# Hybrid decoder step in two-part float32: which engine makes the weights' low parts and the sums of squares

## The chip, the cores and the metric

One core of one Trainium2 chip runs the whole program. The metric is the device time of one execution in microseconds (us); the median of three runs is given. Engines are named as the profile names them: PE (TensorE), DVE (VectorE), ACT (ScalarE), POOL (GpSimd) and SP (the queue from which most transfers start).

## The reference

One inference step of a decoder of two layers, for a prompt of 1024 tokens and 8 sample tokens together (1032 columns), 1024 features, everything in float32. Each layer has two sublayers:

```python
h = modulate(rmsnorm(x, g_mix), sh1, sc1)
p = h @ w_in                      # 1024 -> 3072: q, k, v, g of 4 retention heads; u, vv of 4 gMLP groups
...                               # retention with rotary q/k and group norm; chunked spatial gating
x = x + gt1[:, None, :] * (concatenate([o_ret, o_gm], -1) @ w_out)
h2 = modulate(rmsnorm(x, g_ffn), sh2, sc2)
a, buf_new = causal_dwconv(h2 @ w_up, conv_buf, conv_w, conv_b)   # 1024 -> 4096, width 3
f = jax.nn.silu(a[..., :D_FF]) * a[..., D_FF:]
x = x + gt2[:, None, :] * (f @ w_down)                            # 2048 -> 1024
```

The shifts, scales and gates come from a small product `silu(c) @ w_ada` per layer. After the second layer a last rmsnorm gives the output; the retention states, the convolution states and some rows of the gMLP are outputs too.

## The kernel before

Features lie on the 128 partitions and tokens along the free axis, so X is 8 tiles of 128 x 1032. A product in float32 is made of three products in float32r: each operand is split into a high part (a copy rounded to float32r, made on ScalarE) and a low part (the operand less the high part), and high x high, high x low and low x high are added up in PSUM. `block` does that for one 128x128 weight tile over three token chunks of 344 columns: nine matmuls.

Weights arrive as 160 pieces of eight 128x128 tiles (128 x 1024 columns, 512 KB). The class `Weights` sends for them (`issue`, two pieces ahead, on SP's queue), splits them (`prepare`: the high part on ScalarE at L188, the low part on GpSimd at L189) and hands them out by units (`get`). `ahead` prepares one more piece of the unit that comes next, if it lacks one. It is called in `unit` after k-tiles 2, 4 and 6 of eight, in `partial` at the outputs from the fourth on, in `joint` once, and in `final_partial` after each group of outputs of the second and third chunk. Most units are one piece.

The order of all work is written out by hand, and every engine runs its instructions in that order. A main stream of matrix products runs through the layer; side work (rotary embedding, retention, gating, the convolution's taps) is cut into steps, and `side.tick` puts some between the products. A step says how long, in us of the main stream, the next is to be left alone.

- `unit`: one piece, eight k-tiles, 72 matmuls into one of two PSUM buffers of three banks. Its evacuation starts with a small copy on ScalarE (L596) and a product with the rows' scale on VectorE (L597). In the feed-forward part two ScalarE passes follow, then the taps L887 and the eight sample columns L891 on VectorE, Silu (L901) on ScalarE, the gate L911, and the split into `ahi` (L913) and `alo` (L915).
- `partial`: some k-tiles of a product back to the residual, for all eight outputs; VectorE adds each into X (L299, L305).
- `final_partial`: the last k-tiles of a sublayer, one token chunk after the other (order 2, 0, 1), outputs in groups of three, three and two. VectorE adds them into X (L508). `scaled` makes the next operand: Hh on ScalarE (L411), Hl on VectorE (L412); for output tile 0 ScalarE makes a copy first and GpSimd the low part (L409). `squares` squares each group on ScalarE (L334), and GpSimd adds the first two groups (L338). Then `norm` follows as a side task: `add_squares` adds what is left to one row per partition on VectorE (L345, L353, L357), `inv_rms` sums the row over partitions with four small matmuls (L365) and takes the inverse root on VectorE, and the result goes over DRAM to all partitions as R.
- `joint`: the first two units of the next sublayer, chunk by chunk, so that they can begin before the last chunk is normed; both are evacuated at its end. There are four joints, one per sublayer.
- At the start the same steps are done for X as loaded: `scaled` (no tile on GpSimd there), `squares` (first two chunks on GpSimd, L332, the third on ScalarE), `add_squares`, and between the chunks of the first joint (`start`) the norms and the first part of the conditioning.

Of the kernel before, what the change touches and what calls it, by code (L numbers as in the profile page):

```python
# [7 lines left out]
F32 = mybir.dt.float32  # L8
F32R = mybir.dt.float32r
# [8 lines left out]
NB = 8  # L18
# [13 lines left out]
# columns of the packed per-layer parameters  # L32
# [3 lines left out]
# The k-tiles of the two projections back to the residual, in groups that go into PSUM together.  # L36
# Mixing: 0-3 retention heads, 4-7 gMLP groups.
# [4 lines left out]
POOL_LO = (0,)  # L42
# [13 lines left out]
class Side:  # L56
    """Work that is interleaved with the main stream of matrix products. A task yields how long (in us of the main
    stream) its next step is to be left alone, since it needs what other engines make of the last one."""
# [12 lines left out]
    def tick(self, us):  # L71
        """us of the main stream have been put down: a step of each of the first tasks that are due"""
# [19 lines left out]
def tile_hybrid_decoder_step(  # L92
# [36 lines left out]
    # ---------------------------------------------------------------- constants and state  # L129
# [17 lines left out]
    # ---------------------------------------------------------------- weight stream  # L147
# [37 lines left out]
    def split(t, n, eng=nc.vector):  # L185
        """t of float32 in two float32r parts"""
        hi, lo = slot("hi", F32R), slot("lo", F32R)
        nc.scalar.activation(out=hi[:, 0:n], in_=t[:, 0:n], func=ACTF.Copy)  # L188
        eng.tensor_tensor(out=lo[:, 0:n], in0=t[:, 0:n], in1=hi.bitcast(F32)[:, 0:n], op=ALU.subtract)  # L189
        return hi, lo  # L190

    class Weights:
        """Weights come in pieces of eight 128x128 tiles, are split exactly in two float32r parts,
        and are handed out a unit of the main stream at a time."""

        def __init__(self):
            self.raw, self.split = {}, {}
            self.issued = self.done = self.n = self.unit = 0
# [7 lines left out]

        def prepare(self):
            i = self.done
            self.issue(i + 1)
            self.split[i] = split(self.raw.pop(i), 1024, nc.gpsimd)  # L210
            self.done += 1
            self.issue(self.done + RAW)

        def ahead(self, keep=0):
            """split one more piece of the unit that comes next, if it lacks one"""
            if self.unit < len(units) and self.done < self.n + units[self.unit] - keep:
                self.prepare()
# [31 lines left out]
    def block(ps, whi, wlo, rhi, rlo, start, stop, last=0):  # L249
        """ps[:, c] += (whi + wlo)^T (rhi + rlo) over the three token chunks."""  # L250
# [18 lines left out]
    def joint(evacs, norms, order, ready):  # L269
        """Two units, one token chunk after the other, so that they start with the first chunk."""  # L270
# [17 lines left out]
    def partial(acts, gt, first):  # L288
        """X += gate * (a few k-tiles of the product), all output tiles."""
# [22 lines left out]
    # ---------------------------------------------------------------- norms  # L312
    def rsqrt(x, y, t):
        """y = 1 / sqrt(x / RS): a guess from the bits, a step of second and one of third order"""
# [12 lines left out]
    def squares(c, ms, hold, mul=None, add=nc.gpsimd):  # L327
# [3 lines left out]
        if mul:  # L331
            mul.tensor_tensor(out=o, in0=x, in1=x, op=ALU.mult)  # L332
        else:
            nc.scalar.activation(out=o, in_=x, func=ACTF.Square)  # L334
        hold.append(t)
        if add and len(hold) == 2:
            a, b = hold
            add.tensor_tensor(out=a[:, :, 0:n], in0=a[:, :, 0:n], in1=b[:, :, 0:n], op=ALU.add)  # L338

    def add_squares(c, hold, gate=None):  # L340
        """the chunk's squares, added to one row per partition"""
# [3 lines left out]
        tt(out=d[:, 0:2, 0:n], in0=a[:, 0:2, 0:n], in1=d[:, 0:2, 0:n], op=ALU.add)  # L345
# [823 lines left out]
```

## Time and profile before

| | |
|---|---|
| median of 3 runs | 2128.18 us (2126.92 to 2129.64) |
| profiled execution, first to last instruction (its span) | 2126.2 us |
| TensorE busy with matmuls | 2048.0 us, 96% |
| VectorE, ScalarE, GpSimd busy | 58%, 31%, 25% |
| DMA | 77 GB/s on average |

The profiled execution has no time of its own beside its span: all durations come from these 2126.2 us, which lie 2.0 us under the median of the runs. A group of the profile has a line of the program, an engine, what is written and read, a count, the busy time, the mean of one in ns, and the engine's idle time before these instructions with what ended it.

### The profile page before, as it was taken

The page shows a single profiled execution, that of the slowest core. Times are in us where ns is not written, and L with a number is a line of the kernel's source. Part 1 is how long each engine was busy: PE and PEld are TensorE (multiplying, and loading weights), DVE is VectorE, ACT ScalarE, POOL GpSimd, SP SyncE. Part 2 cuts the span into 40 slices and gives each one's busy share as a digit, 9 for nine tenths or more (in the row PEclk, how much of TensorE's full clock was granted, in tenths as well). Part 3 has the DMA queues.
Part 4 walks back from the last instruction along what each step waited for, and adds up shares of the span by engine and source line. Part 5 has one row for each costly group of instructions (what it writes and reads, how often), then busy time and mean ns, then how long its engine had stood idle before and what let it go on. Part 6 is the DMA issues. An engine that isn't in the chain of part 4 may idle for free. (4 is left out here: it accounts for less than half of the span.)

```text
span 2126.2 us, 31966 instructions
## 1 busy us (share of the span) xinstructions
PE 2048.0 (96%) x13582; PEld 1966.5 (92%) x13582; DVE 1229.5 (58%) x1923; ACT 661.3 (31%) x906; POOL 527.4 (25%) x343
## 2 busy tenths in 40 slices
PE   6899999999999999999999999999999999999997
PEld 3789999988888999999989999999999999999997
DVE  6335725578354556454683665357756555654576
ACT  3222223324322223323443331333333322232332
POOL 5121212233111112121332221323322211212232
PEclk9999999999999999999999999999999999999998
DMA  8553112111663111110122111121111111111102
GB/s 317 189 180 111 50 51 71 52 48 42 236 237 129 41 50 41 40 60 31 50 67 76 62 54 48 62 71 51 41 47 60 40 40 57 43 41 50 40 34 81
DMA packets 51886, 164.29 MB, mean 77 GB/s; under 512 B 6864, under 2 KB 14384, under 8 KB 51744
## 3 DMA queue, kind: packets, MB, share of 16 engines
q1 hardware_dynamic: 47616, 151.22, 21.0%
q0 software_dynamic: 3728, 10.50, 1.4%
q8 instruction: 107, 1.75, 0.3%
q10 hardware_dynamic: 400, 0.53, 0.1%
q14 instruction: 35, 0.29, 0.0%
HBM read 152.88 MB, written 9.61 MB: 76 GB/s over the span
## 5 line engine op out<-in xcount | busy, mean ns | idle before, releaser
L189 POOL TENSOR_TENSOR lo<-raw,hi 128x1024 fp32r<-128x1024 f32 x160 | 411.1, 2572 | 1327.0 <-ACT hi L188 856.2
L254 PE MATMUL big<-Hh,hi 128*128 128x344 f32 (+1 forms) x2496 | 549.0, 328 | 1.9 <-DVE v L597 1.9
L254 PE MATMUL big<-Hh,lo 128*128 128x344 f32 (+1 forms) x2496 | 531.7, 321 | 0.0
L254 PE MATMUL big<-Hl,hi 128*128 128x344 f32 (+1 forms) x2496 | 531.4, 321 | 0.0
L254 PEld LDWEIGHTS big<-Hh,hi 128*128 128x128 f32 x2496 | 413.1, 189 | 31.7 <-issue 28.2
L254 PEld LDWEIGHTS big<-Hh,lo 128*128 128x128 f32 x2496 | 422.0, 189 | 0.0
L254 PEld LDWEIGHTS big<-Hl,hi 128*128 128x128 f32 x2496 | 421.9, 189 | 0.0
L887 DVE SCALAR_TENSOR_TENSOR c<-a,pars,c 128x1032 f32<-128x1032 f32 x128 | 235.0, 1839 | 117.7 <-ACT acol L880 96.9
L299 DVE SCALAR_TENSOR_TENSOR X<-big,mod,X 128x1032 f32<-128x1032 f32 x128 | 165.0, 1289 | 108.4 <-PE big L254 108.4
L597 DVE TENSOR_TENSOR a<-big,R 128x1032 f32<-128x1032 f32 x64 | 78.9, 1233 | 250.7 <-ACT wb L596 161.4
L596 ACT ACTIVATE wb<-big 128x1 f32<-128x1 f32 x112 | 18.8, 168 | 614.9 <-PE big L254 565.2
L188 ACT ACTIVATE hi<-raw 128x1024 fp32r<-128x1024 f32 x160 | 166.7, 1047 | 15.7 <-PE side L557 10.6
L254 PE MATMUL big<-ahi,hi 128*128 128x344 f32 x624 | 134.7, 324 | 14.3 <-DVE a L597 13.6
L254 PE MATMUL big<-alo,hi 128*128 128x344 f32 x624 | 132.2, 320 | 0.0
L254 PE MATMUL big<-ahi,lo 128*128 128x344 f32 x624 | 131.8, 319 | 0.0
L254 PEld LDWEIGHTS big<-ahi,hi 128*128 128x128 f32 x624 | 103.0, 188 | 23.0 <-DVE a L597 16.7
L254 PEld LDWEIGHTS big<-alo,hi 128*128 128x128 f32 x624 | 104.7, 188 | 0.3 <-DVE alo L915 0.3
L254 PEld LDWEIGHTS big<-ahi,lo 128*128 128x128 f32 x624 | 104.4, 188 | 0.0
L913 ACT ACTIVATE ahi<-c 128x1032 fp32r<-128x1032 f32 x32 | 34.2, 1068 | 221.8 <-DVE c L911 221.8
L877 ACT ACTIVATE a<-a,wb 128x1032 f32<-128x1032 f32 x64 | 74.2, 1159 | 84.5 <-DVE a L597 84.5
L412 DVE SCALAR_TENSOR_TENSOR Hl<-X,mod,Hh 128x344 fp32r<-128x344 f32 (+1 forms) x87 | 85.4, 1042 | 1.5 <-ACT Hh L411 1.5
L878 ACT ACTIVATE c<-a,pars 128x1032 f32<-128x1032 f32 x64 | 80.0, 1250 | 3.2
(206 smaller groups left out, 2576.2 us busy)
## 6 DMA issues: line engine op xcount, KB each, us to landing
ada<-in_w_ada SPq DMA_DIRECT2D x96, 512.0 KB, 5.4
raw<-in_w_up SPq DMA_DIRECT2D x64, 512.0 KB, 3.4
raw<-in_w_in SPq DMA_DIRECT2D x48, 512.0 KB, 3.4
raw<-in_w_down SPq DMA_DIRECT2D x32, 512.0 KB, 3.5
raw<-in_w_out SPq DMA_DIRECT2D x16, 512.0 KB, 3.5
S<-in_s_ret POOLq DMA_DIRECT2D x8, 512.0 KB, 3.9
vb<-vd SPq DMA_DIRECT2D x8, 512.0 KB, 4.7
out_rs<-S POOLq DMA_DIRECT2D x8, 512.0 KB, 2.9
```

Of the source, the lines that this page charges most:

```text
L188: nc.scalar.activation(out=hi[:, 0:n], in_=t[:, 0:n], func=ACTF.Copy)
L189: eng.tensor_tensor(out=lo[:, 0:n], in0=t[:, 0:n], in1=hi.bitcast(F32)[:, 0:n], op=ALU.subtract)
L254: nc.tensor.matmul(ps[:, c, 0:n], w, r[:, s], start=st, stop=sp_)
L299: nc.vector.scalar_tensor_tensor(out=v3(X[:, m]), in0=ps[:, :, 0:CW], scalar=gt[:, m, 0:1], in1=v3(X[:, m]), op0=ALU.mult, op1=ALU.add)
L412: late.append(lambda x=x, a=a, m=m: nc.vector.scalar_tensor_tensor(out=Hl[:, m, s], in0=x, scalar=a, in1=Hhf[:, m, s], op0=ALU.mult, op1=A ...
L596: nc.scalar.activation(out=b, in_=ps[:, 2, CW:CW + 1], func=ACTF.Copy)
L597: nc.vector.tensor_tensor(out=v3(a), in0=ps[:, :, 0:CW], in1=v3(R), op=ALU.mult)
L877: nc.scalar.activation(out=a[:, 0:T], in_=a[:, 0:T], func=ACTF.Identity, bias=b)
L878: nc.scalar.activation(out=c[:, 0:T], in_=a[:, 0:T], func=ACTF.Identity, scale=w[2], bias=col(l, P_CB + i))
L887: nc.vector.scalar_tensor_tensor(out=c[:, off:off + T], in0=a[:, 0:T], scalar=wt, in1=c[:, off:off + T], op0=ALU.mult, op1=ALU.add)
L913: nc.scalar.activation(out=hi[:, 0:T], in_=c2[:, 0:T], func=ACTF.Copy)
```

## The change

Low parts of weights are made on VectorE, and `prepare` becomes two calls: `high` (ScalarE) and `low` (VectorE). `ahead` finishes the low part that an earlier call left open, and then starts the next high part. A low part is thus issued one call of `ahead` after its high part, or when the unit is asked for. GpSimd's part of `scaled` goes: all eight low parts are VectorE's. All squares are ScalarE's, all additions of them VectorE's. `add_squares` no longer adds down to one row: three rows remain, and `inv_rms` sums all three over partitions, with twelve small matmuls instead of four.

```diff
-POOL_LO = (0,)
...
-    def split(t, n, eng=nc.vector):
+    def split(t, n):
...
-        eng.tensor_tensor(out=lo[:, 0:n], in0=t[:, 0:n], in1=hi.bitcast(F32)[:, 0:n], op=ALU.subtract)
+        nc.vector.tensor_tensor(out=lo[:, 0:n], in0=t[:, 0:n], in1=hi.bitcast(F32)[:, 0:n], op=ALU.subtract)
...
+        def high(self):
+            i = self.started
+            self.issue(i + 1)
+            hi = slot("hi", F32R)
+            nc.scalar.activation(out=hi[:, 0:1024], in_=self.raw[i][:, 0:1024], func=ACTF.Copy)
+            self.split[i] = [hi]
+            self.started += 1
+            self.issue(self.started + RAW)
+
+        def low(self):
+            i = self.done
+            lo = slot("lo", F32R)
+            nc.vector.tensor_tensor(
+                out=lo[:, 0:1024], in0=self.raw.pop(i)[:, 0:1024], in1=self.split[i][0].bitcast(F32)[:, 0:1024],
+                op=ALU.subtract)
+            self.split[i].append(lo)
+            self.done += 1
+
         def prepare(self):
-            i = self.done
-            self.issue(i + 1)
-            self.split[i] = split(self.raw.pop(i), 1024, nc.gpsimd)
-            self.done += 1
-            self.issue(self.done + RAW)
-
-        def ahead(self, keep=0):
-            if self.unit < len(units) and self.done < self.n + units[self.unit] - keep:
-                self.prepare()
+            if self.started == self.done:
+                self.high()
+            self.low()
+
+        def ahead(self):
+            if self.done < self.started:
+                self.low()
+            if self.unit < len(units) and self.started < min(self.n + units[self.unit], len(pieces)):
+                self.high()
...
-    def squares(c, ms, hold, mul=None, add=nc.gpsimd):
+    def squares(c, ms, hold, add=True):
...
-        if mul:
-            mul.tensor_tensor(out=o, in0=x, in1=x, op=ALU.mult)
-        else:
-            nc.scalar.activation(out=o, in_=x, func=ACTF.Square)
+        nc.scalar.activation(out=o, in_=x, func=ACTF.Square)
         hold.append(t)
         if add and len(hold) == 2:
             a, b = hold
-            add.tensor_tensor(out=a[:, :, 0:n], in0=a[:, :, 0:n], in1=b[:, :, 0:n], op=ALU.add)
+            nc.vector.tensor_tensor(out=a[:, :, 0:n], in0=a[:, :, 0:n], in1=b[:, :, 0:n], op=ALU.add)
...
-        tt(out=d[:, 0:2, 0:n], in0=a[:, 0:2, 0:n], in1=d[:, 0:2, 0:n], op=ALU.add)
+        tt(out=a[:, 0:2, 0:n], in0=a[:, 0:2, 0:n], in1=d[:, 0:2, 0:n], op=ALU.add)
...
-        tt(out=d[:, 0, 0:n], in0=d[:, 0, 0:n], in1=d[:, 1, 0:n], op=ALU.add)
-        if c == 2:
-            nc.vector.tensor_reduce(
-                out=a[:, 2, n:CW], in_=q.rearrange("p m b -> p b m"), axis=AX.X, op=ALU.add)
-        tt(out=a[:, 2, 0:n], in0=d[:, 0, 0:n], in1=a[:, 2, 0:n], op=ALU.add)
-        return [a[:, 2]]
+            for j, ms in enumerate(((0, 1, 2), (3, 4, 5), (6, 7))):
+                nc.vector.tensor_reduce(
+                    out=a[:, j, n:CW], in_=q[:, ms[0]:ms[-1] + 1].rearrange("p m b -> p b m"), axis=AX.X, op=ALU.add)
+        return [a[:, 0], a[:, 1], a[:, 2]]
...
-    def scaled(c, ms, A, late, pool=POOL_LO):
+    def scaled(c, ms, A, late):
...
-            if m in pool:
-                tm = t[:, j, 0:n]
-                nc.scalar.activation(out=tm, in_=x, func=ACTF.Copy, scale=a)
-                nc.scalar.activation(out=Hh[:, m, s], in_=tm, func=ACTF.Copy)
-                nc.gpsimd.tensor_tensor(out=Hl[:, m, s], in0=tm, in1=Hhf[:, m, s], op=ALU.subtract)
-            else:
...
-                squares(c, ms, hold, None, nc.gpsimd if out is None or o < 2 else None)
+                squares(c, ms, hold, out is None or o < 2)
...
-        W.ahead()
+        W.prepare()
...
-                if c == 0 and ms[0] == 0:
-                    W.ahead()
+                    W.prepare()
...
-                squares(c, ms, holds[c], nc.gpsimd if c < 2 else None, nc.vector if c == 2 else nc.gpsimd)
+                squares(c, ms, holds[c])
```

## Rows read from the trace of the kernel before

**Rows 1.** Busy us, share of the span and count of instructions, by engine.

```profile
PE 2048.0 (96%) x13582; PEld 1966.5 (92%) x13582; DVE 1229.5 (58%) x1923; ACT 661.3 (31%) x906; POOL 527.4 (25%) x343
```

**Rows 2.** Busy us of each engine in stretches; TensorE clock, DMA share, GB/s.

```profile
0.00:75.00 75.00, 48.65 (x325) 34.20 (x325) 47.41 (x73) 21.42 (x42) 29.93 (x24) 0.98 0.81 294
...
472.00:536.00 64.00, 59.02 (x374) 57.44 (x373) 45.87 (x94) 26.63 (x44) 19.50 (x14) 0.95 0.18 63
536.00:1037.00 501.00, 497.43 (x3291) 466.41 (x3290) 265.79 (x238) 149.76 (x196) 101.30 (x69) 1.00 0.26 91
```

**Rows 3.** TensorE's waits in the whole span: us in total, times, longest us.

```profile
PE big L254 <- DVE a L597: 13.6, 10, 1.7
PE side L365 <- DVE sq L357: 13.3, 7, 3.9
...
PE big L254 <- DVE ACS L305: 6.5, 5, 2.4
...
PE big L241 <- DVE X L508: 5.9, 6, 1.0
```

**Rows 4.** Groups by line, costliest first.

```profile
L189 POOL TENSOR_TENSOR lo<-raw,hi 128x1024 fp32r<-128x1024 f32 x160 | 411.1, 2572 | 1327.0 <-ACT hi L188 856.2
...
L887 DVE SCALAR_TENSOR_TENSOR c<-a,pars,c 128x1032 f32<-128x1032 f32 x128 | 235.0, 1839 | 117.7 <-ACT acol L880 96.9
```

**Rows 5.** Single lines: least, median and most ns; first and last start.

```profile
L887 DVE SCALAR_TENSOR_TENSOR c<-a,pars,c x128: 1279/1296/3456, 538.0 to 2060.2; 128x1032 f32<-128x1032 f32 x128
...
L189 DVE TENSOR_TENSOR lo<-mix,hi x16: 1232/1234/2515, 190.1 to 1505.4; 128x1032 fp32r<-128x1032 f32 x16
...
L412 DVE SCALAR_TENSOR_TENSOR Hl<-X,mod,Hh x87: 556/566/2751, 22.5 to 1554.6; 128x344 fp32r<-128x344 f32 x58, 128x336 fp32r<-128x336 f32 x29
...
L357 DVE TENSOR_TENSOR sq<-sq,sq x14: 496/516/1109, 54.8 to 2101.7; 128x344 f32<-128x344 f32 x9, 128x336 f32<-128x336 f32 x5
```

**Rows 6.** Timelines of the start: start us, us, instruction, [idle before, releaser].

```profile
19.48 2.41 DVE L580 SCALAR_TENSOR_TENSOR mod<-mod,pars 128x72 f32<-128x72 f32 x1
...
24.91 25.05 DVE L412 SCALAR_TENSOR_TENSOR Hl<-X,mod,Hh 128x344 fp32r<-128x344 f32 x21 [0.82 <-ACT Hh L411]
...
26.98 7.62 ACT L411 ACTIVATE Hh<-X,mod 128x344 fp32r<-128x344 f32 x16 [0.22 <-DMA X<-in_xT]
34.50 2.63 ACT L334 ACTIVATE sq<-X 128x1008 f32<-128x1008 f32 x3
...
55.69 0.52 PE L365 MATMUL side<-sq,ones_m 128*32 128x86 f32 x8 [3.94 <-DVE sq L357]
```

**Rows 7.** Timelines around a feed-forward partial product, by engine.

```profile
756.35 2.54 POOL L189 TENSOR_TENSOR lo<-raw,hi 128x1024 fp32r<-128x1024 f32 x1 [3.22 <-ACT hi L188]
...
756.51 2.40 DVE L891 SCALAR_TENSOR_TENSOR c<-a,pars,cbs 128x8 f32<-128x8 f32 x1
...
759.00 1.07 ACT L901 ACTIVATE c<-c 128x1032 f32<-128x1032 f32 x1 [2.73 <-DVE c L891]
...
761.45 0.74 PE L254 MATMUL big<-ahi,hi 128*128 128x344 f32 x3 [1.63 <-DVE a L597]
```

**Rows 8.** Timelines in a partial product of the mixing.

```profile
444.99 2.43 DVE L325 SCALAR_TENSOR_TENSOR fac<-fact,fac 128x9 f32<-128x9 f32 x1
...
448.83 0.71 PE L254 MATMUL big<-hi,hi 128*128 128x344 f32 x3 [2.39 <-DVE ACS L305]
```

**Rows 9.** VectorE's timeline at a sublayer's end.

```profile
497.18 5.90 DVE L412 SCALAR_TENSOR_TENSOR Hl<-X,mod,Hh 128x344 fp32r<-128x344 f32 x5
```

**Rows 10.** Timelines behind a joint's end.

```profile
536.04 0.64 PE L254 MATMUL big<-Hh,hi 128*128 128x344 f32 x3
...
537.00 0.63 PE L254 MATMUL big<-Hh,lo 128*128 128x344 f32 x3
...
536.81 1.23 DVE L597 TENSOR_TENSOR a<-big,R 128x1032 f32<-128x1032 f32 x1 [2.72 <-ACT wb L596]
```

**Rows 11.** TensorE's timeline: sums over partitions.

```profile
2109.26 0.65 PE L365 MATMUL side<-sq,ones_m 128*32 128x86 f32 x24
```

More of the change, by code (lines that the diff above doesn't have):

```diff
@@ L197, in __init__ @@
             self.raw, self.split = {}, {}
-            self.issued = self.done = self.n = self.unit = 0
+            self.issued = self.started = self.done = self.n = self.unit = 0
         def issue(self, upto):
@@ L396, in columns @@
         nc.vector.tensor_tensor(out=Hl[:, :, t], in0=b, in1=Hhf[:, :, t], op=ALU.subtract)
-    def scaled(c, ms, A, late, pool=POOL_LO):
+    def scaled(c, ms, A, late):
         n = CW if c < 2 else CW - NB
         s = slice(c * CW, c * CW + n)
-        t = v3(slot("nt")) if any(m in pool for m in ms) else None
-        for j, m in enumerate(ms):
+        for m in ms:
             a, x = A[:, m, 0:1], X[:, m, s]
-            if m in pool:
-                tm = t[:, j, 0:n]
-                nc.scalar.activation(out=tm, in_=x, func=ACTF.Copy, scale=a)
-                nc.scalar.activation(out=Hh[:, m, s], in_=tm, func=ACTF.Copy)
-                nc.gpsimd.tensor_tensor(out=Hl[:, m, s], in0=tm, in1=Hhf[:, m, s], op=ALU.subtract)
-            else:
-                nc.scalar.activation(out=Hh[:, m, s], in_=x, func=ACTF.Copy, scale=a)
-                late.append(lambda x=x, a=a, m=m: nc.vector.scalar_tensor_tensor(
-                    out=Hl[:, m, s], in0=x, scalar=a, in1=Hhf[:, m, s], op0=ALU.mult, op1=ALU.subtract))
+            nc.scalar.activation(out=Hh[:, m, s], in_=x, func=ACTF.Copy, scale=a)
+            late.append(lambda x=x, a=a, m=m: nc.vector.scalar_tensor_tensor(
+                out=Hl[:, m, s], in0=x, scalar=a, in1=Hhf[:, m, s], op0=ALU.mult, op1=ALU.subtract))
     def norm(c, hold, R, A, B, gate=None, dma=True):
@@ L957, in tile_hybrid_decoder_step @@
                 late = []
-                scaled(c, ms, A, late, ())
+                scaled(c, ms, A, late)
                 for f in late:
```

## Prediction

> **What bounds the kernel now.** I read the busy shares first, then busy time stage by stage, then TensorE's waits, then the durations behind those waits. TensorE's matrix products are busy 2048.0 of 2126.2 us [rows 1], so at most 78 us of idle TensorE time can be won, and every matmul that is added counts. The stages show where the idle time lies [rows 2]: 26 us in the first 75 us, 5 us in the 64 us around a sublayer's end (three such places in the kernel), 3.6 us in 501 us of feed-forward work. The waits name who TensorE waits for [rows 3]: VectorE in nearly all of them, as the evacuation L597 (13.6 us in ten waits), as the row of squares L357 (13.3 us), as the sums L305 and L508 (12.4 us together).
>
> Why VectorE is late is in the durations. L887 reads two tensors from SBUF; it takes 1.28 us at best, 1.30 in the median, yet 1.84 on average and 3.46 at worst [rows 4, 5]. The surplus falls where GpSimd subtracts at L189: an update of eight columns (L891) starts 0.16 us after a GpSimd subtraction and ends with it, 2.40 us long [rows 7]. So VectorE stands still until GpSimd's instruction is over. GpSimd does 160 of them at 2.57 us [rows 4]. The reader is to see that a GpSimd instruction nobody waits for stretches VectorE instructions that TensorE does wait for.
>
> **The change, part by part.** Six terms; negative is time saved.
>
> *1. Start.* Now the scale L580 takes 2.41 us for 72 columns, and 21 products L412 take 25.05 us, 1.19 each, against 0.566 in the median [rows 5, 6]. The row of squares for the first norm is ready only after 55 us, with TensorE 3.94 us in wait of it [rows 6]. After the change GpSimd does none of this. I walk it anew: the scale is ready near 19.8 instead of 21.9; ScalarE makes a chunk's eight high parts at 0.48 (7.62 over 16), 3.9 us, and then three squares, 2.6 us, which it now does for all chunks; with one high part of weights (about 1 us, by the squares' rate) it is through at 19.8 + 1 + 3 x 6.5 = 40.3 at the earliest, say 40.7, and the second chunk's data, there at 27.0, hold nothing up. VectorE trails it: low parts of weights and additions of squares are 1.23 each (the same operation at that width is 1.234 in rows 5), L412 0.57. After the last square come one addition of 0.86 (an estimate for 672 columns from L357's 0.52 for half of them) and three small reductions, two of them new, 0.8 together (each put at half an L357, since it reads a fifth of its columns): about 43 instead of 55.6. TensorE, fed by then, needs 7.7 us for a chunk's 48 matmuls at 0.16 us (six in 0.96) [rows 10] and gets there at 41 to 44. Gain 12.4, less three sums of rows (term 6): **-11**. Bounds: -6 if TensorE's clock stays low as long as now, -13.
>
> *2. Feed-forward partial products.* At ten places TensorE waits up to 1.7 us for L597, 13.6 in all [rows 3]. [Rows 7] show the chain: the stretched L891 ends at 758.9, ScalarE's Silu L901 waits for it and keeps the small copy behind it waiting, that copy holds L597, and TensorE goes on at 761.45. Without the stretch L891 is through over 2 us earlier. But two low parts at 1.23 now stand in VectorE's queue before it, and the second waits for a high part that itself waits on ScalarE behind another step. By that order L891 ends near 757.3, TensorE's wait shrinks from 1.6 to 0.4: 8 full places times 1.2: **-10**. Bounds -5 and -13.6.
>
> *3. Partial products of the mixing.* The last step of a reciprocal root (L325, nine columns) takes 2.43 us beside three low parts on GpSimd, and TensorE waits 2.39 us [rows 8]. All such waits (L305) sum to 6.5 [rows 3]. After the change the three low parts follow in program order, after the sums of outputs 4 to 6, where an output's 18 matmuls give VectorE 2.9 us for a sum of about 1.3 (an estimate, from 1.23 at that width) and a low part. **-5**; bounds -2 and -6.5.
>
> *4. The last partial product of a sublayer, three times.* Here VectorE is the limit: 45.9 us busy in 64 [rows 2], TensorE waits 9.4 us for L357 (13.3 less the 3.94 at the start) and 5.9 for L508 [rows 3]. It gains the stretch: a chunk's L412 run at 1.18 (five in 5.90) and will run at 0.57 [rows 5, 9], and two additions of 0.52 go. It loses: one more L412 a chunk (it was GpSimd's), an addition of squares of 1.2, a low part of 1.2 in the middle chunk for each of two pieces. Over the three chunks: 21 products between 0.57 and 1.18 against 24 at 0.57 give -11 to +2, say -5; six additions less, -3.1; against three additions, +3.7, two or three low parts, +3.1, and reductions, +0.5: nearly zero. But the additions and low parts stand in front of evacuations that TensorE waits for. Walked through in order, TensorE's wait for the second sum of rows ends 0.4 us later than now, two sums of rows included; a third of 0.5 comes on top. **+2.7** for the three. Bounds -8 and +8.
>
> *5. New waits.* The joint start of a sublayer calls for the next piece of weights once. Now that call makes both parts; after the change only the high part. The low part is issued when the next unit asks for it, behind both evacuations in VectorE's queue. In [rows 10] the second evacuation runs from 536.81 to 538.04; the low part would end at 539.27. TensorE wants it for its third block of the unit, now at 537.00, so it waits 2.25. All four joint starts are built so, one evacuation behind the other; I take 2.1 each: **+8.4**. It could be 0 only if VectorE were early there, which the row excludes; upper bound 9.
>
> *6. Three rows summed instead of one.* Each of 14 norms gets eight more small matmuls, 16 records; 24 records take 0.65 us [rows 11], so 0.43 to 0.5 each. Start and sublayer ends have theirs above; two at the end of the kernel: **+0.9**.
>
> What stays hidden: of 160 low parts some 100 belong to units of one piece. Such a low part goes out at the fifth of eight k-tiles (5.8 us into the 11.5 of 72 matmuls), and is wanted 0.96 us into the next unit, so 6.7 us cover 1.23. Raw tiles are held one call longer and nine scratch tiles fall away; transfers on SP's queue still start two pieces ahead. POOL's queue holds its DMAs, which now wait behind less.
>
> Sum: -11 - 10 - 5 + 2.7 + 8.4 + 0.9 = -14.0 against a span of 2126.2, so 2112.2. The median of the runs lies 2.0 above that span; on its scale **2114.2**.
>
> The Trainium skill, Perfetto Trace Analysis (Optimizing Scalar/DVE Operations), advises to offload from a saturated VectorE to GpSimd, but warns that the two share a read port of SBUF, so that moving work between them may not help. Its first half speaks against this change, and would turn term 4 into the rule (the second rival); its second half is what rows 7 show.
>
> **The rivals.**
>
> *No change: TensorE's clock eats the gain.* Where TensorE had waited, the rows show a lower granted clock: 0.95 over the 64 us of a sublayer's end, so 3.2 us of work lost, against 1.00 over the 501 us after it [rows 2]. If each of the four new waits brings as much, that is +12.8, and the time is 2127. For it: that stretch, where TensorE waited 5 us. Against: those 501 us hold 3.6 us of idle time in pieces of under 2 us and keep 1.00. The Trainium skill, TensorE: Matmul & The Clock Gate (What's actually happening), says that the clock is halved by how busy the array has recently been; by that rule the waits that go would give some back too.
>
> *Slower: VectorE's queue becomes the limit.* VectorE runs in order. If it is more than 5.5 us behind TensorE (6.7 less 1.23) at the fifth k-tile, every unit of one piece starts with a wait. There are 104 such units; 0.3 us each is +31, and the time 2145. For it: the crowded 64 us of rows 2. Against: 266 of 501 us busy in the feed-forward work, with the stretch in it. It decides from 0.13 us a unit on.
>
> *Larger gain.* The sublayer ends lose most of their 15 us of waits and the stretches in terms 2 and 3 go wholly: -13 - 13.6 - 6.5 - 8 + 8.4 + 0.9 = -32, 2096.
>
> *The stretch is not GpSimd's doing.* Then 160 times 1.23 come on top for nothing; rows 7 make that very unlikely. It would be slower, near 2150.
>
> **How the numbers follow.** Forecast 0.58 (2104 to 2123), clock 0.14, VectorE's queue 0.14, larger gain 0.12, the last 0.02. A measurement here tells 0.2% (4.3 us) from no change. Faster: 0.58 + 0.12 and a little of the clock case, 0.72; same 0.13; slower 0.15. The range goes from 2101, into the larger gain, to 2128, the clock case.
>
> **What the profile after would show.** L887 near 1.29 and L412 near 0.57 at mean, GpSimd under 100 us: the lock is gone. The sum of rows at the start near 43: term 1. TensorE's waits for L597 near 4 us: term 2. Four waits of about 2 us for the low part at the first unit after a joint start: term 5. Wrong would make me: waits for low parts in many units, more half clock, or sublayer ends that change by more than 8 us.

## The result, and the profile after

The kernel after takes 2097.65 us (median of four runs, 2096.24 to 2099.05), beside 2127.55 us (2126.74 to 2129.64) for the kernel before on the same chip: a ratio of 0.9854, 95% interval 0.9841 to 0.9866. The forecast, 2114.2 us with a range from 2101 to 2128, had the direction and less than half of the gain; the result lies 3.4 us below the range. The profiled execution's span is 2094.5 us, 31.7 less than before's 2126.2; most of the texts below go by spans, because places of a trace can be compared.

The page's busy times of the kernel after, by engine, as in [rows 1]:

```profile
PE 2045.0 (98%) x13806; PEld 1967.1 (94%) x13806; DVE 1172.9 (56%) x2087; ACT 663.0 (32%) x903; POOL 69.8 (3%) x155
```

VectorE took over 160 subtractions and became less busy by 57 us. The groups by line of the same kernel, and two single lines with least, median and most ns (L220 is the new low part, L895 the tap that was L887, L420 the low part of the operand that was L412; compare [rows 4] and [rows 5]):

```profile
L220 DVE TENSOR_TENSOR lo<-raw,hi 128x1024 fp32r<-128x1024 f32 x160 | 195.0, 1219 | 63.5 <-ACT hi L211 63.5
...
L895 DVE SCALAR_TENSOR_TENSOR c<-a,pars,c 128x1032 f32<-128x1032 f32 x128 | 165.0, 1290 | 111.9 <-ACT acol L888 85.9 <-ACT c L886 24.8 <-issue 1.2
```

```profile
L895 DVE SCALAR_TENSOR_TENSOR c<-a,pars,c x128: 1282/1289/1297, 523.1 to 2027.3; 128x1032 f32<-128x1032 f32 x128
...
L420 DVE SCALAR_TENSOR_TENSOR Hl<-X,mod,Hh x96: 555/568/575, 19.9 to 1528.1; 128x344 fp32r<-128x344 f32 x64, 128x336 fp32r<-128x336 f32 x32
```

The tap's most is now 1.30 us where it was 3.46, and the operand's low part never exceeds 0.575 us. In both the stretch is gone.

TensorE's waits in the whole span, as in [rows 3]:

```profile
PE side L565 <- DMA ada<-in_w_ada: 8.3, 7, 5.6
PE big L274 <- DVE lo L220: 7.2, 4, 1.8
PE big L261 <- DVE X L516: 6.0, 8, 1.7
...
PE side L380 <- DVE sq L362: 3.4, 3, 1.1
...
PE big L274 <- DVE ACS L325: 1.4, 2, 0.7
```

The feed-forward evacuation into `a` (L597, now L605) is no longer in the list: its ten waits of 13.6 us are gone. The row of squares fell from 13.3 to 3.4, the sums of the mixing from 6.5 to 1.4. New are four waits for the low part of a piece, 7.2 us.

The stretches that answer to [rows 2], moved forward by what was won ahead of them (us of the stretch, then busy time of PE, PEld, DVE, ACT and POOL, TensorE's clock, DMA share, GB/s):

```profile
0.00:63.00 63.00, 47.95 (x377) 36.18 (x378) 30.08 (x74) 27.77 (x49) 5.17 (x13) 0.99 0.92 343
457.00:521.00 64.00, 61.55 (x432) 59.58 (x433) 42.76 (x101) 26.11 (x43) 4.76 (x11) 0.97 0.22 72
521.00:1015.00 494.00, 492.16 (x3264) 461.91 (x3263) 249.91 (x277) 148.96 (x191) 2.81 (x28) 1.00 0.27 90
```

TensorE is idle for 15 us of the start instead of 26, 2.5 instead of 5.0 at the sublayer's end, 1.8 instead of 3.6 in the feed-forward work.

**Where the time came from.** Both traces hold the same 11,520 products of the main stream in the same order, so each has its partner, and the difference of their starts is a curve that moves only where one kernel gains or loses (negative is time saved). Read along the stream, against the six terms of the prediction:

| term | forecast | curve |
|---|---|---|
| 1 start | -11 | -12.1 |
| 2 feed-forward partial products | -10 | -17.0 (eight steps of 1.87 to 1.98, two of 0.57) |
| 3 mixing partial products | -5 | -7.7 (up to 1.7 of it lower clock that went) |
| 4 the three sublayer ends | +2.7 | -4.8 |
| 5 four waits behind joints | +8.4 | +9.9 (1.8, 2.15, 2.2, 3.7; 1.7 of the last is lower clock) |
| 6 sums of rows at the kernel's end | +0.9 | +0.1 |
| sum | -14.0 | -31.6 |

Where one term ends and the next begins is a choice, and small steps of the curve lie on the borders (0.8 to 0.9 at the first products of each sublayer's end, 0.6 just before the second sublayer end and the kernel's end, 0.9 of lower clock at the first joint). Cut strictly at the first product of each part of the code, the same curve reads -13.3, -18.3, -8.3, -3.0, +10.5 and +0.8. Signs and order are the same; a difference of 1 or 2 us between terms is not to be read.

The same lines at the places of [rows 6] to [rows 10], from timelines of the kernel after (start us, us, instruction, idle time before it and its releaser), VectorE and ScalarE first:

```profile
18.61 0.23 DVE L588 SCALAR_TENSOR_TENSOR mod<-mod,pars 128x72 f32<-128x72 f32 x1
...
28.93 3.99 DVE L420 SCALAR_TENSOR_TENSOR Hl<-X,mod,Hh 128x344 fp32r<-128x344 f32 x8
...
434.09 0.17 DVE L345 SCALAR_TENSOR_TENSOR fac<-fact,fac 128x9 f32<-128x9 f32 x1
...
500.25 2.52 DVE L420 SCALAR_TENSOR_TENSOR Hl<-X,mod,Hh 128x344 fp32r<-128x344 f32 x5
...
520.85 1.23 DVE L605 TENSOR_TENSOR a<-big,R 128x1032 f32<-128x1032 f32 x1 [2.66 <-ACT wb L604]
522.00 1.22 DVE L220 TENSOR_TENSOR lo<-raw,hi 128x1024 fp32r<-128x1024 f32 x1
...
739.23 1.04 ACT L211 ACTIVATE hi<-raw 128x1024 fp32r<-128x1024 f32 x1
...
741.62 1.22 DVE L220 TENSOR_TENSOR lo<-raw,hi 128x1024 fp32r<-128x1024 f32 x1
742.76 0.22 DVE L899 SCALAR_TENSOR_TENSOR c<-a,pars,cbs 128x8 f32<-128x8 f32 x1
```

and TensorE's:

```profile
42.94 0.65 PE L380 MATMUL side<-sq,ones_m 128*32 128x86 f32 x24
...
435.68 0.71 PE L274 MATMUL big<-hi,hi 128*128 128x344 f32 x3 [0.70 <-DVE ACS L325]
...
490.46 0.65 PE L380 MATMUL side<-sq,ones_m 128*32 128x86 f32 x24 [1.11 <-DVE sq L362]
...
520.31 0.64 PE L274 MATMUL big<-Hh,hi 128*128 128x344 f32 x3
520.79 0.63 PE L274 MATMUL big<-Hl,hi 128*128 128x344 f32 x3
523.27 0.74 PE L274 MATMUL big<-Hh,lo 128*128 128x344 f32 x3 [1.84 <-DVE lo L220]
...
745.82 0.62 PE L274 MATMUL big<-ahi,hi 128*128 128x344 f32 x3
```

The scale takes 0.23 us (2.41), the last step of the root 0.17 (2.43), eight columns of samples 0.22 (2.40), five low parts 2.52 (5.90). The sums of rows at the start run at 42.94 without a wait, forecast near 43. At 745.82, the place of the 1.63 us wait of [rows 7], there is none. At 523.27 stands one of the four new waits, with the low part that it waits for right behind the joint's second evacuation.

### The profile page after: what moved, and what is told of

Same layout as the page of the kernel before. It is cut to its first block, busy times and chain, and to the rows that moved or that the text cites. A ratio compares the mean times of both kernels' runs of the same rounds, so it can differ in the third digit from the quotient of the medians.

```text
span 2094.5 us, 32222 instructions
## 1 busy us (share of the span) xinstructions
PE 2045.0 (98%) x13806; PEld 1967.1 (94%) x13806; DVE 1172.9 (56%) x2087; ACT 663.0 (32%) x903; POOL 69.8 (3%) x155
## 4 chain that ended last, share of the span: by engine, by line
PE 88%; DVE 7%; ACT 2%; issue 1%; DMA 1%; POOL 0%; SPq 0%; POOLq 0%; DVEq 0%; ACTq 0%
PE big L274 75%; PE side L565 2%; PE big L262 2%; PE big L261 2%; PE big L263 2%; PE side L614 1%; DVE X L516 1%; DVE lo L220 1%; ACT Hh L419 1%; DVE Hl L420 1%; ACT sq L351 1%; PE side L726 1%; PE side L777 1%; PE side L755 1%; PE side L779 1%
## 5 line engine op out<-in xcount | busy, mean ns | idle before, releaser
L274 PEld LDWEIGHTS big<-Hh,hi 128*128 128x128 f32 x2496 | 413.9, 190 | 31.7 <-issue 28.2
L220 DVE TENSOR_TENSOR lo<-raw,hi 128x1024 fp32r<-128x1024 f32 x160 | 195.0, 1219 | 63.5 <-ACT hi L211 63.5
L605 DVE TENSOR_TENSOR a<-big,R 128x1032 f32<-128x1032 f32 x64 | 78.9, 1233 | 269.3 <-ACT wb L604 269.3
L895 DVE SCALAR_TENSOR_TENSOR c<-a,pars,c 128x1032 f32<-128x1032 f32 x128 | 165.0, 1290 | 111.9 <-ACT acol L888 85.9
L211 ACT ACTIVATE hi<-raw 128x1024 fp32r<-128x1024 f32 x160 | 166.6, 1047 | 19.7 <-PE big L274 16.6
L565 PE MATMUL side<-ada,scond 128*32 128x256 f32 x768 | 64.1, 413 | 8.5 <-DMA ada<-in_w_ada 8.3
```

The lines of the kernel that those rows point to most:

```text
L211: nc.scalar.activation(out=hi[:, 0:1024], in_=self.raw[i][:, 0:1024], func=ACTF.Copy)
L220: nc.vector.tensor_tensor(out=lo[:, 0:1024], in0=self.raw.pop(i)[:, 0:1024], in1=self.split[i][0].bitcast(F32)[:, 0:1024], op=ALU.subtract)
L274: nc.tensor.matmul(ps[:, c, 0:n], w, r[:, s], start=st, stop=sp_)
L565: nc.tensor.matmul(ps[32 * j:32 * j + 32, 0:256], scond[:, k, :], w[:, j * 256:(j + 1) * 256], start=(k == 0), stop=(k == KT - 1), tile_po ...
L605: nc.vector.tensor_tensor(out=v3(a), in0=ps[:, :, 0:CW], in1=v3(R), op=ALU.mult)
L895: nc.vector.scalar_tensor_tensor(out=c[:, off:off + T], in0=a[:, 0:T], scalar=wt, in1=c[:, off:off + T], op0=ALU.mult, op1=ALU.add)
```

## The experiments

Each kernel ran beside the kernel before; the ratio is to that. The last column adds up the trace's records of the lower of TensorE's two clock levels (1.2 instead of 2.4 GHz), without the last 10 to 14 us of the kernel, where all are at it. At most half of it is time lost: TensorE is not busy in all of it, and at two sublayer ends the loss does not show in the time (see the clock rival below).

| kernel | median us | ratio, 95% interval | span us | us at the lower level |
|---|---|---|---|---|
| before | 2127.55 | 1 | 2126.2 | 23.9 |
| after | 2097.65 | 0.9854 [0.9841, 0.9866] | 2094.5 | 13.7 |
| weights_low_on_vectore_only | 2108.7 | 0.9907 [0.9892, 0.9922] | 2106.3 | 20.5 |
| three_rows_only | 2120.68 | 0.9953 [0.9936, 0.9969] | 2117.4 | 27.3 |
| weights_low_on_gpsimd | 2111.17 | 0.9921 [0.9906, 0.9935] | 2107.7 | 6.8 |
| gpsimd_low_one_behind | 2110.47 | 0.9904 [0.9883, 0.9924] | 2110.1 | 17.1 |
| one_row | 2108.55 | 0.9905 [0.9889, 0.9922] | 2107.7 | 37.5 |
| squares_on_gpsimd | 2103.12 | 0.9870 [0.9854, 0.9886] | 2101.2 | 13.7 |
| low_in_same_call | 2129.6 | 1.0003 [0.9992, 1.0014] | 2126.2 | 30.7 |
| gpsimd_reads | 2211.5 | 1.0396 [1.0378, 1.0413] | 2208.9 | 102.4 |
| gpsimd_writes | 2103.75 | 0.9891 [0.9876, 0.9906] | 2106.9 | 30.7 |
| joint_low_in_time | 2086.87 | 0.9808 [0.9794, 0.9823] | 2086.0 | 10.2 |
| joint_and_gpsimd_adds | 2085.37 | 0.9800 [0.9786, 0.9813] | 2082.9 | 6.8 |
| joint_and_gpsimd_at_ends | 2080.55 | 0.9777 [0.9764, 0.9791] | 2078.5 | 3.4 |

**Is it GpSimd's reading that holds VectorE? (gpsimd_reads, gpsimd_writes)** The kernel after, with GpSimd given work that nobody uses: in the first the old subtraction into a scratch tile, in the second two fills of a scratch tile.

```diff
+            dum = slot("dum")
+            nc.gpsimd.tensor_tensor(out=dum[:, 0:1024], in0=self.raw[i][:, 0:1024],
+                in1=self.split[i][0].bitcast(F32)[:, 0:1024], op=ALU.subtract)
```
```diff
+            dum = slot("dum")
+            for _ in range(2):
+                nc.gpsimd.memset(dum[:, 0:1024], 0.0)
```

> The changed kernel, and GpSimd again subtracts every weight piece, into a scratch tile that nobody reads: 160 instructions that take nothing over from VectorE. Theory A (a GpSimd instruction that reads SBUF holds up VectorE instructions with two SBUF inputs until it ends): the tap L895 goes from 1.29 back towards 1.8 us at mean, the waits at the feed-forward partial products come back, and since VectorE now carries the low parts as well the time goes to 2115 to 2150. Theory B (the gain came from the new order and from fewer steps, not from GpSimd being empty): within 5 us of the changed kernel, 2093 to 2103.

> The changed kernel, and GpSimd clears a scratch tile of the same size twice per weight piece: about the same GpSimd busy time, the same scratch tile held, but no read of SBUF. Theory A in the form that only reads matter: the tap stays at 1.29 us and the time within 5 us of the changed kernel, 2093 to 2103. Theory A in the form that any GpSimd instruction blocks: as with the reading one, 2110 or more. Theory B: as the changed kernel.

The groups by line of gpsimd_reads, with two of its TensorE waits behind them in a fence of their own:

```profile
L224 DVE TENSOR_TENSOR lo<-raw,hi 128x1024 fp32r<-128x1024 f32 x160 | 287.4, 1796 | 62.3 <-ACT hi L211 57.9 <-issue 2.2 <-DMA ada<-in_w_ada 2.2
...
L923 DVE TENSOR_TENSOR c<-c,c 128x1032 f32<-128x1032 f32 x32 | 76.7, 2397 | 0.0
...
L220 POOL TENSOR_TENSOR dum<-raw,hi 128x1024 f32<-128x1024 f32 x160 | 439.8, 2750 | 1425.8 <-ACT hi L211 1015.6 <-issue 305.6 <-PE big L278 27.5
```

```profile
PE big L278 <- DVE a L609: 41.4, 12, 4.7
PE big L278 <- DVE lo L224: 14.0, 8, 2.3
```

and of gpsimd_writes:

```profile
L223 DVE TENSOR_TENSOR lo<-raw,hi 128x1024 fp32r<-128x1024 f32 x160 | 195.2, 1220 | 63.7 <-ACT hi L211 63.7
...
L898 DVE SCALAR_TENSOR_TENSOR c<-a,pars,c 128x1032 f32<-128x1032 f32 x128 | 165.1, 1291 | 111.9 <-ACT acol L891 81.4 <-ACT c L889 28.0 <-issue 2.5
...
L221 POOL MEMSET dum<- 128x1024 f32 x320 | 305.5, 955 | 1061.4 <-PE big L277 402.9 <-DVE lo L223 220.7 <-DVE c L922 150.3
```

and four lines of its timelines, with a place where fills do hold VectorE up:

```profile
431.51 6.03 POOL L221 MEMSET dum<- 128x1024 f32 x6 [10.85 <-PE big L277]
435.61 0.94 DVE L633 TENSOR_SCALAR facx<-mv 128x9 f32<-128x9 f32 x1
436.58 0.99 DVE L339 TENSOR_SCALAR fac<-facx 128x9 int32<-128x9 int32 x1
440.42 0.71 PE L277 MATMUL big<-hi,hi 128*128 128x344 f32 x3 [2.31 <-DVE ACS L328]
```

160 subtractions on GpSimd stretch VectorE's low part from 1.22 to 1.80 us at mean and cost 114 us, far above either expectation. 306 us of GpSimd fills leave the low part and the tap, which have two inputs in SBUF, as they were: 1.220 and 1.291. So for these it is what GpSimd reads, not that it is busy. The fills cost 12 us by spans, 6 by medians (2103.75, just above what either theory gave for fills that hold nothing up). At most 8.5 of the 12 are lower clock (half of 30.7 less 13.7), and 3.2 are longer waits of TensorE for L328 (4.6 where after has 1.4, L325 there). The cause of these is in the lines above: the two instructions of nine columns have a single input, and take 0.94 and 0.99 us while GpSimd fills, where after has 0.18 and 0.17 (432.45 and 432.66); TensorE's wait is 1.6 us longer there (0.70 at 435.68 in after). So a fill does hold up some of VectorE's instructions. Whether the scratch tile, taken from the pool of the kernel's own tiles, costs something too was not tried apart.

**The engine or the distance? (weights_low_on_gpsimd, gpsimd_low_one_behind, low_in_same_call)** Three edits of the kernel after: the low part on GpSimd, right behind the high part as before the change, or one call behind it as after; and on VectorE, but right behind the high part.

```diff
-            if self.done < self.started:
-                self.low()
...
-                self.high()
+                self.prepare()
```
```diff
-            nc.vector.tensor_tensor(out=lo[:, 0:1024], ...
+            nc.gpsimd.tensor_tensor(out=lo[:, 0:1024], ...
```

The first has both edits, the second the lower one, the third the upper one.

> The changed kernel with the low parts of weights back on GpSimd, in the same call as the high part; squares, their additions, all of Hl and the three rows stay as changed. Theory A: most of the stretch is back outside the sublayer ends: the ten waits at the feed-forward partial products (16.9 us of the gain) and those of the mixing (7.7) return, the four new waits (8.1) go, and about half of the start's 12 stays: 2108 to 2118. Rival (the gain is that of the norms: squares, scaled operands and three rows): 2090 to 2100.

> The kernel after with only the weights' low parts back on GpSimd, still one call of ahead behind the high part. Theory (VectorE held by GpSimd's reads is what costs; the distance of a call costs GpSimd nothing): about as with the low parts on GpSimd in the same call (2111.2), 2106 to 2115, the taps' mean near 1.84 us and TensorE's waits for the evacuations of the feed-forward units back at 9 us or more. Rival (the gain came from the distance, not from the engine): within 4 us of the kernel after, 2094 to 2102.

> The changed kernel with each low part issued right behind its high part, in the same call of ahead, as the kernel before did it on GpSimd. The four waits behind the joints go, since the single call there makes both parts: -8 to -11 us as in the run joint_low_in_time. Against that VectorE, which takes its instructions in order, waits for ScalarE's copy each time: if that costs TensorE nothing, 2086 to 2090; if the wait stands in front of evacuations, as one call behind is meant to avoid, 2092 to 2110, with waits back at the feed-forward partial products.

On GpSimd the distance makes no difference (2111.2 and 2110.5; the tap's mean 1.842 and 1.853 us, TensorE's waits for the evacuation back at 13.5 and 13.8). On VectorE it is worth 32 us, the whole of the change, more than either theory gave. VectorE's idle time in low_in_same_call, by what it waited for, and then timelines of the next place of the kind of [rows 7], 71 us behind the one that answers to it (there, from 738.78 to 747.07, the same instructions show the same waits to 0.01 us):

```profile
DVE lo L220 <- ACT hi L211: 278.5, 94, 6.1
```

```profile
810.13 1.07 ACT L919 ACTIVATE ahi<-c 128x1032 fp32r<-128x1032 f32 x1 [3.64 <-DVE c L917]
811.10 1.04 ACT L211 ACTIVATE hi<-raw 128x1024 fp32r<-128x1024 f32 x1
...
812.18 1.23 DVE L220 TENSOR_TENSOR lo<-raw,hi 128x1024 fp32r<-128x1024 f32 x1 [2.08 <-ACT hi L211]
813.32 1.29 DVE L893 SCALAR_TENSOR_TENSOR c<-a,pars,c 128x1032 f32<-128x1032 f32 x1
...
815.67 0.22 DVE L897 SCALAR_TENSOR_TENSOR c<-a,pars,cbs 128x8 f32<-128x8 f32 x1
...
815.99 1.07 ACT L907 ACTIVATE c<-c 128x1032 f32<-128x1032 f32 x1 [3.84 <-DVE c L897]
...
818.43 0.75 PE L272 MATMUL big<-ahi,hi 128*128 128x344 f32 x3 [1.41 <-DVE a L603]
```

The high part stands on ScalarE behind a copy (L919) that itself waited 3.64 us for VectorE. The low part stops VectorE for 2.08 us in the middle of its work, with a tap, `alo` and the sample columns behind it, Silu waits for these, the evacuation for Silu's engine, TensorE for the evacuation. In the kernel after, the low part at 741.62, of the place that answers to [rows 7], starts 1.35 us after its high part has ended, and waits for nothing. VectorE's idle time for high parts is 278.5 us here and 63.5 after; TensorE waits 19.7 us for evacuations into `a` (none after) and 15.1 for the sums L514 (6.0 after, L516 there). So two engines that run in order and feed each other in both directions need the distance; GpSimd, which had nothing behind the low part that anyone waited for, did not.

**What each part is worth (weights_low_on_vectore_only, three_rows_only, one_row, squares_on_gpsimd)** The first two put one part into the kernel before: the class `Weights` of after with its two calls of `prepare`; `add_squares` of after. The other two take one part out of the kernel after: `add_squares` of before; `squares`, `scaled` and their calls of before.

> The kernel before, and only the low parts of weights go to VectorE, one call behind; squares, their additions, one tile of Hl on GpSimd and the single row stay. By place in the stream: feed-forward partial products -16.9, mixing -7, joints +8.1, start -3 (the squares on GpSimd still hold up VectorE there): about -19, 2105 to 2112. If the parts of the change add up exactly (before less the run with the weights' low parts on GpSimd is -16.6, the whole change -30): -13.5, 2113 to 2116.

> The kernel before with only the three rows: no additions down to one row, twelve small products instead of four. If the parts add up: 11 us under the kernel before, 2114 to 2119. Rival: with GpSimd still in the chain of squares the row's last additions are not what TensorE waits for longest, and the gain is 0 to 6 us: 2121 to 2128. The prediction's step 4 and 6 had the extra sums as a cost of 0.5 us each.

> The changed kernel, but the squares are added down to one row per partition on VectorE again, and four matmuls instead of twelve sum it over partitions. The three rows are worth, by the prediction, two additions of 0.52 us less on VectorE against 0.45 us more on TensorE per norm, so nearly nothing: 2095 to 2101. Rival (the gain at the sublayer ends, 4.8 us where I had forecast a loss of 2.7, comes from the two additions that stood between TensorE and its sum): 2101 to 2108, with TensorE's waits for the sum of rows back from 3.4 towards 9 us.

> The kernel after with its squares, their first additions and output tile 0's low parts as in the kernel before (GpSimd, and at the start GpSimd makes the squares of two chunks); weights on VectorE and three rows stay. If the parts add up (31 in all, 13.5 for the weights, 11 for the three rows), some 6 us remain for this part: 2101 to 2107, nearly all of it in the first 80 us. Rival: the start alone is worth the 12 us that it gained: 2107 to 2114.

By spans, taking out the weights costs 13.2 us (15.6 with the distance kept), the three rows 13.2, the squares 6.7: 33 to 36 in all, where the change has 31.7. By medians it is 13.5 (12.8), 10.9 and 5.5, which add up to the change's 29.9 within 1 us. Putting in alone, the weights give 19.9 and the rows 8.8. Two of the four expectations came true (weights_low_on_vectore_only and squares_on_gpsimd, by their theories); three_rows_only fell between its two ranges, and one_row came out 0.55 us above its rival's. The curve of one_row against after loses 4.7 us at the start, 7.2 at the three sublayer ends and the joints behind them, and 0.7 behind the last of the stream's norms. Its mean clock is lower: the span and mean granted clock of it, and of after:

```profile
core 0: 2107.7 us, clock 0.988
```

```profile
core 0: 2094.5 us, clock 0.994
```

TensorE waits 5.5 us longer for the row of squares (8.9 instead of 3.4), and at most 11.9 us, half of 37.5 less half of 13.7, can be lost to the lower level around these places; the two together are more than the 13.2 us of the run, so not all of the 11.9 was lost. All four executions of one_row have 0.988. That the longer waits bring the lower clock is what the places suggest; no run sets the clock by itself.

squares_on_gpsimd loses 11.7 us at the start, and gains 5.6 at the three sublayer ends. The part is right at the start and wrong later.

**What the result pointed to (joint_low_in_time, joint_and_gpsimd_at_ends, joint_and_gpsimd_adds)** The joint calls `ahead` once more, at its last chunk, so that the low part goes out ahead of the evacuations:

```diff
-            if o == 1:
+            if o >= 1:
                 W.ahead()
```

The second kernel also gives GpSimd back, at the sublayer ends and the last norm alone, the first additions of squares and the low part of output tile 0 (`scaled` of before comes back for that, not shown); the third only the additions, with an empty `POOL_LO`.

```diff
+POOL_LO = (0,)
...
-                squares(c, ms, hold, out is None or o < 2)
+                squares(c, ms, hold, None, nc.gpsimd if out is None or o < 2 else None)
...
-                squares(c, ms, holds[c])
+                squares(c, ms, holds[c], None, nc.vector)
```

> The changed kernel, and a joint start calls for the next piece once more, after its third chunk, so that the low part of the next unit stands in VectorE's queue ahead of the two evacuations. Theory A with the new wait as I have it (the low part behind both evacuations costs about 2 us at each of four joints): the four waits for the low part, 7.2 us in all, go, and one drop of the clock may go with them: 7 to 11 us less than the changed kernel, 2087 to 2091. Rival (TensorE would wait there anyway, for an evacuation or for R): 0 to 3 us less.

> The kernel after with two edits: the joint's call for the low part made one chunk earlier than the unit asks for it (as in joint_low_in_time), and, at the sublayer ends and the last norm only, GpSimd again adds the first two groups of squares and makes output tile 0's low part; the start stays as after. Theory from the run squares_on_gpsimd (at the three sublayer ends those few GpSimd instructions relieve VectorE by more than they hold it, 5 us less than after behind the start): 2080 to 2084. Rival (those 5 us were changes of TensorE's clock and of the joint's wait, not VectorE's relief): 2085 to 2091, that is, no better than joint_low_in_time at 2086.9.

> As joint_and_gpsimd_at_ends, but output tile 0's low parts stay on VectorE, so that GpSimd only adds squares (13 additions of about 2.5 us). If the additions are what relieves VectorE at the sublayer ends: 2081 to 2085; if the low part of tile 0 is: 2086 to 2090.

The first loses all four waits for low parts; its curve gains 2.8, 2.1, 1.9 and 3.7 at the four joints, where the shown waits were 7.2 in sum; up to 1.7 of the last is less time at the lower clock, and 1.0 of the first it had lost just before, at that level. At 2086.87 it lies at the fast edge of its Theory A. The second is the fastest of all, 2080.55 us, 0.9777 of before, inside its theory's range. Its nine low parts and eleven additions on GpSimd, from its groups by line:

```profile
L359 POOL TENSOR_TENSOR sq<-sq,sq 128x1032 f32<-128x1032 f32 (+1 forms) x11 | 27.6, 2511 | 78.4 <-ACT sq L355 78.4
...
L428 POOL TENSOR_TENSOR Hl<-nt,Hh 128x344 fp32r<-128x344 f32 (+1 forms) x9 | 8.3, 922 | 51.3 <-ACT Hh L427 48.7 <-DMA raw<-in_w_up 2.6
```

The additions alone (third kernel, 2085.37, between its two forecasts) give 1.5 us against joint_low_in_time by medians, which its interval does not tell from nothing; the low parts give 4.8 more. Of the 7.5 us by spans between the first and the second, the curve puts 1.6 at the start, where both run the same code and only the first has a stretch at the lower level, so that part is luck. It puts 1.8, 2.0 and 1.8 at the three sublayer ends, and at the first two of them neither kernel has such a stretch; so the relief of VectorE is shown there. The wait that goes there is one of 1.6 us for L516, behind the second sum of rows.

## Why the prediction was wrong in size

**The mechanism held.** A GpSimd instruction that reads SBUF stops VectorE's instructions with two SBUF inputs until it ends: L891's 2.40 us in [rows 7] became 0.22, and gpsimd_reads brought the stretch back with a subtraction that nobody uses. The Trainium skill, SBUF — State Buffer (Who interferes with whom), says that a VectorE instruction with two SBUF inputs contends with a GpSimd instruction that reads SBUF, and not with one that only writes there; the two runs agree, with 1.796 and 1.220 us for the same low part. The rival that the stretch was not GpSimd's doing falls, and so does the one of VectorE's queue: no unit of one piece in the feed-forward work waits for its low part, and all four waits lie behind joints.

**Terms 1, 5 and 6 held.** The start gave 12.1 where 11 stood, with the sums of rows at 42.94. The four waits were foreseen by place, cause and, at 8.4 against 8.2 without the 1.7 of lower clock at the last, by price; joint_low_in_time took them away by the one call that the term blamed.

**Term 2 was mis-sized, 7.0 us.** Two steps failed. The walk left 0.4 us of wait at eight places because the second low part would wait for its high part; it waits for nothing (741.62), and the sample columns end at 742.98, on before's time 756.83 where the walk had 757.3. And the price of a wait was read off its row. A wait is counted from the modelled end of the last product, and products overlap: after 523.27's wait of 1.84 the stream is 2.00 late, since the next group of three would have started 0.48 after 520.79, and the first group behind a wait takes 0.74 instead of 0.63. So 1.6 us of shown wait cost 1.87 to 1.98 each on the curve, and the 13.6 us in [rows 3] were worth 16.6; two smaller places of 0.57 each were not counted. Term 3 is off in the same way, -7.7 against 6.5 of shown waits, with up to 1.7 us of lower clock that went with them.

**Term 4 had the wrong sign, 7.5 us.** The step that failed is "TensorE's wait for the second sum of rows ends 0.4 us later than now, two sums of rows included; a third of 0.5 comes on top". At the first sublayer end the second sum of rows runs at 490.46, on before's time 504.1 instead of 506.31: 2.2 us earlier. VectorE, which starts its two evacuations there 1.1 later than before with a low part in front, needs 3.8 us for five products and a low part of weights (1.54 + 1.22 + 1.05) where it needed 5.90 for five stretched products, and then has one addition before the sum instead of three. What the walk got wrong was above all the three rows. Cut strictly at the first product of the last partial product and at the end of the joint, the ends stand at +2.0 in one_row against before (0.7, 0.1 and 1.1) and at -3.0 in after (-1.3, -1.1 and -0.7): with one row they are near the +2.7 of the term, and the three rows are worth 5.0 there. The two small additions were booked at their 0.52 us of VectorE, 3.1 for six, the extra products at 0.5 each. They stand last in a chain that ends in a wait of TensorE: that wait (for L357, now L362) is 2.9 us at each end before, 2.2 in one_row and 1.1 in after. The cost that the term feared is there too: at the second and third ends TensorE now waits 1.6 us for a sum L516 behind the second sum of rows, 1095.56 in the first of them, which no end had before, and the ends would have gained more without it.

**The clock rival had the sign wrong.** It let four new waits cost 12.8 us of lower clock. The clock did fall at two of the four, the first and the last (62.0 and 1550.2), but over the whole kernel the time at the lower level fell from 23.9 to 13.7 us. That gives back 5.1 us of work at most, and how much of it is part of the gain is not shown. At the first sublayer end after spends 3.4 us at the lower level (492.1) and joint_low_in_time none; there TensorE waits 1.6 us for L516 instead, and at the third end it is the other way round, yet the ends agree to 0.2 us. And of the four executions of after, the one with the lowest mean clock, 0.991 where the others have 0.994, has the shortest span, 2094.2 us. The rival "larger gain", -32 with -13 for start, -13.6 and -6.5 for terms 2 and 3 and -8 for the ends, is nearest to what happened. That its sum is met to 0.3 us is luck: term 2 gave 3.4 more than it says and the ends 3.2 less.

## What to carry to other kernels

Price a wait by the stream that it delays, product by product, and not by its row: here a row of 1.6 us was 1.9. Lower clock beside a wait is to be counted only where the stream shows that it was lost. Move work off GpSimd where its reads stretch what the bound engine waits for, but give the engine that takes it a step of distance from an engine that it feeds in turn: the whole change won 31.7 us with the low parts one call behind the high parts, and nothing with both in the same call. And an engine that is cleared of 160 instructions can still take back twenty small ones at the place where VectorE is the limit: the Trainium skill, Perfetto Trace Analysis (Optimizing Scalar/DVE Operations), holds offloading and its doubt about the shared port side by side, and here both show: 160 low parts on GpSimd cost 12.8 us (2110.47 against 2097.65), 20 small instructions at the sublayer ends win 6.3 (2080.55 against 2086.87).

## What the runs showed of the hardware

- A GpSimd subtraction gets longer as well: 2.57 us beside the old VectorE work [rows 4], 2.75 us at mean in gpsimd_reads, where VectorE subtracts the same piece.
- GpSimd fills left VectorE's low parts (1.220 us) and taps (1.291) alone, but small TENSOR_SCALAR instructions (L633 and L339 on nine columns, L848 on eight) took up to 0.94, 0.99 and 1.10 us in gpsimd_writes, where after has at most 0.18, 0.18 and 0.29 for the same ones.
- How much VectorE is stretched says little of the price. In weights_low_on_gpsimd VectorE is busy for 1195.8 us where after, without its 195.0 us of low parts, has 977.9: 218 us of stretch, for 13.2 us of span. In gpsimd_reads it is 1410.1 against 1172.9: 237 us of stretch, for 114 us of span. There 92 us of it fall on the low parts, which stand in front of evacuations in VectorE's queue (TensorE waits 41.4 us for twelve evacuations, 14.0 for low parts), and TensorE spent 102.4 us at the lower clock level instead of 13.7; how the 114 us divide was not tried.
- The lower level showed up in seven places in one_row and in three in after, although TensorE is busy for 97% and 98% of the spans. One trace of each was read, and whether the places repeat from execution to execution stays open; the mean clock of one_row is 0.988 in all four executions, that of before goes from 0.985 to 0.991.
